# Trunk block on one core: x parts kept in DRAM, retention results transposed on VectorE, squares and last stores regrouped

## The chip, the cores and the metric

The kernel runs on one core of a Trainium2 chip. The metric is the device time of one execution in microseconds (us); lower is better. Engines are named as in the profile: PE (TensorE matmuls), PEld (its weight loads), DVE (VectorE), ACT (ScalarE), POOL (GpSimd), SP (SyncE, which here only issues DMAs).

## What is computed

One layer of a hybrid trunk over 16 meta tokens and 4096 tokens of width 1024, in float32. The reference, cut to what matters:

```python
u = _rmsnorm(h, norm_gain[l])
proj = jnp.einsum('btd,de->bte', u, w_in[l])
lru_x, lru_gate, q, k, v, ret_gate = jnp.split(proj, split_idx, axis=-1)
xc = _causal_conv(lru_x, conv_w[l], conv_b[l])
y_lru = _rg_lru(xc, w_rg[l], b_rg[l], w_ig[l], b_ig[l], lru_lambda[l]) * jax.nn.silu(lru_gate)
...
o = _head_norm(_retention(qh, kh, vh), ret_norm_gain[l])
y_ret = o.reshape(B, T, RET_WIDTH).astype(x.dtype) * jax.nn.silu(ret_gate)
y = jnp.concatenate([y_lru, y_ret], axis=-1)
h = h + jnp.einsum('bte,ed->btd', y, w_out[l])
return _rmsnorm(h, final_norm_gain)[:, N_META:]
```

`_retention` works on chunks of 128 tokens with a state that is handed from chunk to chunk; there are 8 heads of 64 (q, k) and 128 (v) columns.

## The kernel before, in words

Every float32 operand of a large product is held as two parts, `hi` (the value rounded to the matmul's format) and `lo` (the rest), and every product is three matmuls (`mm3`: hi·hi, hi·lo, lo·hi, lines L114 to L116). `split` makes the parts, on ACT (hi, L105) and DVE (lo, L106).

The program has three stages. `ph` is 0 or 1, one half of the channels or heads.

1. **LRU stage**, ph 0 (to about 430 us) and ph 1 (to about 862 us). Tokens go in nine tiles of 272, 256 and seven times 512 columns. `load_x` brings a tile's x in four pairs (`xraw`, 512 KB each, L445) and splits them; the parts of a tile are eight buffers of the pool `big` (28 buffers, 24 of which hold weights and x in use). For each of four blocks `b` of 128 channels PE makes `px` and `pg` (24 matmuls each) and the gate products `pgt`. `block_front` and `block_back` run on ACT and DVE, and `tail` stores the results `sg` to `ydram` (L522).
2. **Retention**, ph 0 (862 to about 1490 us) and ph 1 (to about 2130 us), 32 chunks each. `ret_x` brings the chunk's x once more, from a copy in another order (`xraw` from `xt`, 512 KB), and splits it on ACT (L179) and POOL (L180). A chunk is a pipeline: `front_qk`, `front_v`, `front_g` project it (`ps`), `back_s` makes the scores `pS`, `back_o` the output `po` and the state's update `pkv`, then DVE and POOL take the head norm's statistics, ACT writes `on` (L791), `back_g` multiplies it by the gate (`on` by `gs`, DVE L797), and `back_y` transposes `on` with four PE matmuls against the identity (`py`, L804), copies `py` out on ACT (`yt`, L805) and stores it to `ydram` (256 KB). `back_g` and `back_y` are those of the chunk before the last.
3. **Output sweep** (2130 us to the end): y times w_out, with Strassen-like sums, seven products `i` for each pair of row tiles (a `Unit`). Half h = 0 (LRU channels) adds its rows into `hdram` by an accumulating DMA on POOL's queue; half h = 1 (retention channels, from about 2440 us) adds `hdram` to its rows (`h<-hdram`, L346), then takes their squares (ACT, L348), the root (POOL, L349 and L351), the scaling (DVE, L357) and stores them.

A scheduler that models the engines sets the order of the instructions on each engine; `tc.issue_after` ties some to another. All SP DMAs share one queue in issue order and eight semaphore lanes, so that each waits for the one eight before it.

Of the kernel before, what the change touches and what calls it, by code (L numbers as in the profile page):

```python
# [10 lines left out]
F32 = mybir.dt.float32  # L11
# [22 lines left out]
def hybrid_kernel(ctx: ExitStack, tc: tile.TileContext, xa, xt, x, meta, w_in, w_out,  # L34
# [12 lines left out]
    ydram = [dpool.tile([P, 16, P], F32, name=f"ydram{n}") for n in range(NT)]  # L47
# [97 lines left out]
    rws, rxs = {}, {}  # L145

# [18 lines left out]
    def ret_x(ph, n):  # L165
        if (ph, n) not in rxs:
# [75 lines left out]
    class Unit:  # L242
        def __init__(self, h, n0, n1):
            self.h, self.n, self.y, self.raw = h, (n0, n1), {}, None

        def load(self):
            self.raw = []
            for n in self.n:
                t = raws.tile([P, 2, 4, P], F32, tag="raw", name="yraw")
                load(t, ydram[n][:, 8 * self.h:8 * self.h + 8, :].rearrange("p (g k) t -> p g k t", g=2))  # L250
                self.raw.append(t)

        def operand(self, i):
# [16 lines left out]
            return split(src, t[:, 0], t[:, 1])  # L270
# [29 lines left out]
    def combine(u, i):  # L300
# [13 lines left out]
        if late_unit(u):  # L314
            r0, r1 = u.r
            if i == 2:
# [3 lines left out]
                return add(x0[:, :512], r0[:, :512], g[0])  # L320
# [19 lines left out]
    def finished(u, j, sq):  # L340
# [621 lines left out]
```

## Time and profile before

| what | value |
|---|---|
| median of 3 runs (lowest, highest) | 2776.18 us (2774.13, 2776.66) |
| the profiled execution's own time | 2772.7 us |
| its span (first to last instruction) | 2770.9 us |
| busy: PE | 2716.7 us, 98% of the span |
| busy: DVE, ACT, POOL | 2130.1, 1374.0, 544.9 us (77%, 50%, 20%) |
| moved by DMA | 290.10 MB, mean 105 GB/s |

Busy time of PE is the time in which some matmul is under way. The share of an engine over the whole span hides which stage it belongs to, and a row of the timeline tells when an instruction began, how long it took and, in brackets, how long its engine had stood idle ahead of it and who released it.

### The profile page before, as it was taken

What the parts mean: (1) busy time and instruction counts of PE and PEld (TensorE: products, weight loads), DVE (VectorE), ACT (ScalarE), POOL (GpSimd) and SP (SyncE); (2) the same over time, 40 slices, a digit from 0 to 9 for tenths busy, and PEclk for the clock granted to TensorE, in tenths of its full rate; (3) what the DMA queues carried; (4) which work ended last, traced back from release to release, by engine and by line L of the source; (5) the groups of instructions that cost most, each with busy time, mean ns of one, the idle gap of its engine ahead of it and who ended that gap; (6) DMA issues with size and microseconds to landing.
All of it is one profiled execution on the core that took longest, in us unless ns stands there. A gap on an engine that the chain in (4) does not pass through costs nothing.

```text
span 2770.9 us, 37027 instructions
## 1 busy us (share of the span) xinstructions
PE 2716.7 (98%) x13178; PEld 2288.6 (83%) x13178; DVE 2130.1 (77%) x4502; ACT 1374.0 (50%) x2451; POOL 544.9 (20%) x702
## 2 busy tenths in 40 slices
PE   7999999999999999999999999999999999999998
PEld 7788888888888888888888888888887888877886
DVE  7777889878789877777779888888778755566664
ACT  5766666655565444444446544454445422244342
POOL 3101021000003322222222222222221000012222
PEclk9999999999999999999999999999999999999999
DMA  6434334212224222222214222223112745475654
GB/s 197 120 106 121 118 97 122 84 57 67 75 85 145 72 69 72 69 72 69 70 57 164 79 80 83 101 109 114 47 48 77 191 112 111 108 206 162 178 158 116
DMA packets 164411, 290.10 MB, mean 105 GB/s; under 512 B 21201, under 2 KB 89330, under 8 KB 163714
## 3 DMA queue, kind: packets, MB, share of 16 engines
q1 hardware_dynamic: 150690, 238.45, 26.8%
q0 software_dynamic: 13536, 49.29, 8.2%
q8 instruction: 103, 1.69, 0.3%
q14 instruction: 82, 0.67, 0.1%
HBM read 205.87 MB, written 98.58 MB: 110 GB/s over the span
## 4 chain that ended last, share of the span: by engine, by line
PE 80%; DVE 9%; DMA 4%; issue 3%; ACT 2%; POOL 1%; SPq 0%; DVEq 0%; POOLq 0%; ACTq 0%
PE ps L114 12%; PE ps L116 12%; PE ps L115 12%; PE pg L114 3%; PE pg L116 3%; PE pg L115 3%; PE px L116 3%; PE px L114 3%; PE px L115 3%; PE po L764 2%; PE oc L295 2%; PE oc L297 2%; PE od L297 2%; PE oc L296 2%; PE od L296 2%
## 5 line engine op out<-in xcount | busy, mean ns | idle before, releaser
L114 PE MATMUL ps<-cwh,xhi 128*128 128x512 f32 x1536 | 605.7, 394 | 0.6 <-DVE mr L671 0.6
L116 PE MATMUL ps<-cwh,xlo 128*128 128x512 f32 x1536 | 600.4, 391 | 0.7 <-POOL xlo L180 0.7
L115 PE MATMUL ps<-cwl,xhi 128*128 128x512 f32 x1536 | 600.3, 391 | 0.0
L116 PEld LDWEIGHTS ps<-cwh,xlo 128*128 128x128 f32 x1536 | 288.9, 188 | 62.4 <-POOL xlo L180 1.1
L114 PEld LDWEIGHTS ps<-cwh,xhi 128*128 128x128 f32 x1536 | 289.2, 188 | 57.4 <-DVE mr L671 1.0
L115 PEld LDWEIGHTS ps<-cwl,xhi 128*128 128x128 f32 x1536 | 289.2, 188 | 55.8 <-issue 0.2
L634 DVE STREAM_TRANSPOSE pT<-rd 32x128 f32<-32x128 f32 x1024 | 310.0, 303 | 16.4
L180 POOL TENSOR_TENSOR xlo<-xraw,xhi 128x1024 fp32r<-128x1024 f32 x64 | 163.8, 2559 | 529.6 <-ACT xhi L179 523.6
L105 ACT ACTIVATE yop<-yraw 128x512 fp32r<-128x512 f32 x192 | 116.9, 628 | 217.6 <-DVE yraw L264 71.5
L114 PE MATMUL px<-xhi,lwh 128*128 128x512 f32 (+2 forms) x576 | 215.3, 375 | 8.3 <-ACT lwh L108 6.5
L114 PE MATMUL pg<-xhi,lwh 128*128 128x512 f32 (+2 forms) x576 | 212.8, 370 | 3.6 <-DVE sg L492 3.2
L116 PE MATMUL px<-xhi,lwl 128*128 128x512 f32 (+2 forms) x576 | 214.3, 372 | 1.0 <-DVE lwl L106 1.0
L116 PE MATMUL pg<-xhi,lwl 128*128 128x512 f32 (+2 forms) x576 | 212.4, 369 | 2.8 <-DVE lwl L109 1.7
L115 PE MATMUL px<-xlo,lwh 128*128 128x512 f32 (+2 forms) x576 | 213.9, 371 | 1.0 <-DVE xlo L106 0.9
L115 PE MATMUL pg<-xlo,lwh 128*128 128x512 f32 (+2 forms) x576 | 212.2, 368 | 0.0
L475 DVE SCALAR_TENSOR_TENSOR xc<-xlb,vec,xc 128x512 f32<-128x512 f32 (+2 forms) x216 | 155.4, 720 | 30.2 <-ACT xc L472 26.5
L106 DVE TENSOR_TENSOR yop<-yraw,yop 128x512 fp32r<-128x512 f32 x192 | 130.0, 689 | 52.6 <-ACT yop L105 50.7
L791 ACT ACTIVATE on<-po,nb,rs 128x128 f32<-128x128 f32 x256 | 96.3, 457 | 129.7 <-POOL nb L788 129.7
L782 DVE BATCH_NORM_STATS2 bs<-po 128x6 f32<-128x128 f32 x256 | 57.0, 285 | 108.0 <-PE po L764 107.9
L114 PEld LDWEIGHTS px<-xhi,lwh 128*128 128x128 f32 x576 | 110.5, 192 | 26.8 <-ACT lwh L108 6.5
L114 PEld LDWEIGHTS pg<-xhi,lwh 128*128 128x128 f32 x576 | 109.5, 190 | 22.3 <-DVE sg L492 4.3
L115 PEld LDWEIGHTS px<-xlo,lwh 128*128 128x128 f32 x576 | 110.6, 192 | 20.1 <-DVE xlo L106 1.9
(216 smaller groups left out, 6179.8 us busy)
## 6 DMA issues: line engine op xcount, KB each, us to landing
xraw<-in_xt_dram SPq DMA_DIRECT2D x64, 512.0 KB, 4.6
yraw<-ydram SPq DMA_DIRECT2D x64, 512.0 KB, 3.8
xraw<-in_xa_dram SPq DMA_DIRECT2D x56, 512.0 KB, 4.0
hdram<-in_x_dram SPq DMA_DIRECT2D x32, 512.0 KB, 3.9
xn<-in_x_dram SPq DMA_DIRECT2D x32, 512.0 KB, 5.3
ydram<-sg SPq DMA_DIRECT2D x256, 64.0 KB, 1.7
ydram<-yt SPq DMA_DIRECT2D x64, 256.0 KB, 2.4
hdram<-h POOLq DMA_DIRECT2D x32, 512.0 KB, 5.2
```

Of the source, the lines that this page charges most:

```text
L105: nc.scalar.activation(hi, src, AF.Identity)
L106: return nc.vector.tensor_tensor(lo, src, hi.bitcast(F32), op=ALU.subtract)
L114: nc.tensor.matmul(ps, ah, bh, start=start, stop=False)
L115: nc.tensor.matmul(ps, ah, bl, start=False, stop=False)
L116: nc.tensor.matmul(ps, al, bh, start=False, stop=stop)
L180: nc.gpsimd.tensor_tensor(lo, raw, hi.bitcast(F32), op=ALU.subtract)
L296: nc.tensor.matmul(ps, ah, bl, start=False, stop=False, skip_group_check=more)
L297: mm = nc.tensor.matmul(ps, al, bh, start=False, stop=k == 3, skip_group_check=more)
L475: conv = nc.vector.scalar_tensor_tensor(xc[:, :T], xl[:, j:j + T], vec[:, 6 + j, ch:ch + 1], xc[:, :T], op0=ALU.mult, op1=ALU.add)
L634: ins = nc.vector.transpose(dst[32 * g:32 * g + 32, :, 32 * q:32 * q + 32], sv[32 * q:32 * q + 32, :, g, :])
L782: nc.vector.bn_stats(bs[:, h, :], po[:, h, :])
L791: nc.scalar.activation(on[:, h, :], po[:, h, :], AF.Identity, bias=nb[:, h:h + 1], scale=rs[:, h:h + 1])
```

## The change

Five edits come together.

1. *x parts in DRAM.* The eight parts of each 512-column tile are stored to `xsd` (eight 512 KB DMAs per tile, seven tiles in ph 0; the two small tiles follow in ph 1, `keep_x`). In ph 1 the LRU stage loads the parts of the 512-column tiles from there (two DMAs per pair where there was one, no split), and the retention loads both parts of each chunk (two DMAs of 512 KB in runs of 512 bytes, where there were one DMA, an ACT and a POOL instruction).
2. *Zeros first.* DVE clears a buffer, and PE multiplies it 12 times (128x512) ahead of its first real matmul.
3. *Late squares.* In half h = 1 the squares of a unit are issued after the hi part of the product i = 7 of the next (`added`), the last unit takes half of its squares two products earlier, and the last two row tiles are scaled and stored in two column halves, through SP.
4. *Retention results.* The four PE transposes, the ACT copy and the one 256 KB store give way to one DVE instruction that transposes each 32x32 block of the 128x512 tile, and four stores of 64 KB in runs of 128 bytes that put the blocks in their places in `yret`. The rows of w_out and the head norm's gains are put in the matching order on the host. `back_y` is tied to the same place as `back_g`.
5. *Small loads later.* The loads of `tgm`, `dc`, `msk` and `tg` are tied to the last `xraw` load.

The diff, cut to its core:

```diff
-    ydram = [dpool.tile([P, 16, P], F32, name=f"ydram{n}") for n in range(NT)]
+    ydram = [dpool.tile([P, 8, P], F32, name=f"ydram{n}") for n in range(NT)]
+    yret = [[dpool.tile([P, 4, P], F32, name=f"yret{n}_{ph}") for ph in range(2)] for n in range(NT)]
...
@@ ret_x
-                raw = raws.tile([P, KT, P], F32, tag="raw", name="xraw")
-                nc.sync.dma_start(out=raw, in_=xt[n])
-                hi = big.tile([P, KT, P], F32R, tag="b", name="xhi")
-                lo = big.tile([P, KT, P], F32R, tag="b", name="xlo")
-                nc.scalar.activation(hi, raw, AF.Identity)
-                nc.gpsimd.tensor_tensor(lo, raw, hi.bitcast(F32), op=ALU.subtract)
-                rxs[ph, n] = (hi, lo)
+                i = next(j for j, tt in enumerate(ttiles) if n in tt[2])
+                o = (n - ttiles[i][2][0]) * P + (NM if i == 0 else 0)
+                parts = []
+                for s, nm in enumerate(("xhi", "xlo")):
+                    t = big.tile([P, KT, P], F32R, tag="b", name=nm)
+                    nc.sync.dma_start(out=t.bitcast(F32), in_=xsd[i][s][:, :, o:o + P])
+                    parts.append(t)
+                rxs[ph, n] = tuple(parts)
...
@@ Unit.load
-                load(t, ydram[n][:, 8 * self.h:8 * self.h + 8, :].rearrange("p (g k) t -> p g k t", g=2))
+                if self.h == 0:
+                    load(t, ydram[n].rearrange("p (g k) t -> p g k t", g=2))
+                else:
+                    for ph in range(2):
+                        load(t[:, ph], yret[n][ph])
...
@@ combine, late unit, i == 2
-                return add(x0[:, :512], r0[:, :512], g[0])
+                op = add(x0[:, :512], r0[:, :512], g[0])
+                square(u, 1, 1, g[0])
+                square(u, 0, 0, g[0])
+                return op
...
@@ finished
-        if not late_unit(u):
+        if late_unit(u):
+            square(u, j, 1 - j, sq)
+            root(t, n)
+        else:
             nc.gpsimd.dma_start(out=t, in_=hdram[n], accum_op=ALU.add)
-        for c in range(2):
-            nc.scalar.activation(sq, t[:, 512 * c:512 * c + 512], AF.Square, accum_out=es[:, n, c:c + 1])
+            adding.append((u, j, sq))
...
+    def added(mark, keep=0):
+        while len(adding) > keep:
+            u, j, sq = adding.pop(0)
+            with tc.issue_after(mark.ins):
+                for c in range(2):
+                    square(u, j, c, sq)
+            root(u.x[j], u.n[j])
+
-    def end(keep=0):
-        while len(ending) > keep:
+    def end():
+        while ending:
             t, n = ending.pop(0)
-            nc.vector.scalar_tensor_tensor(t, t, er[:, n:n + 1], gb, op0=ALU.mult, op1=ALU.mult)
-            nc.gpsimd.dma_start(out=out[n * P:(n + 1) * P, :], in_=t)
+            parts = 2 if n >= NT - 2 else 1
+            for c in range(parts):
+                cols = slice(c * D // parts, (c + 1) * D // parts)
+                nc.vector.scalar_tensor_tensor(t[:, cols], t[:, cols], er[:, n:n + 1], gb[:, cols],
+                                               op0=ALU.mult, op1=ALU.mult)
+                (nc.gpsimd if parts == 1 else nc.sync).dma_start(out=out[n * P:(n + 1) * P, cols], in_=t[:, cols])
...
@@ steps of the sweep
-            if i == 5 or (i, u.n[0]) == (6, 4):
+            if i == 7 or (i, u.n[0]) == (1, 4):
+                added(u.hi[i], 2 if i == 1 else 0)
+            if i in ((6, 5) if u.n[0] == 4 else (4,)):
                 with tc.issue_after(op.ins):
-                    end(2 if i == 6 else 0)
+                    end()
...
+    xsd = [[dpool.tile([P, KT, tt[1]], F32, name=f"xs{i}_{s}") for s in range(2)]
+           for i, tt in enumerate(ttiles)]
...
@@ load_x
+            if ph == 1 and i > 1:
+                parts = []
+                for s, nm in enumerate(("xhi", "xlo")):
+                    t = big.tile([P, 2, TB], F32R, tag="b", name=nm)
+                    nc.sync.dma_start(out=t[:, :, :T].bitcast(F32), in_=xsd[i][s][:, kk, :])
+                    parts.append(t)
+                return parts
...
+        def keep_x(i, parts):
+            with tc.issue_after(lloads[-1].ins):
+                for k2, pair in enumerate(parts):
+                    for s, t in enumerate(pair):
+                        store.dma_start(out=xsd[i][s][:, 2 * k2:2 * k2 + 2, :], in_=t[:, :, :ttiles[i][1]].bitcast(F32))
...
@@ LRU stage, first tile and each tile's end
+                    wz = big.tile([P, KT, P], F32R, tag="b", name="wz")
+                    nc.vector.memset(wz[:, 0:4, :].bitcast(F32), 0.0)
+                    pz = psp.tile([P, TB], F32, tag="c", name="pz")
+                    for _ in range(12):
+                        nc.tensor.matmul(pz, wz[:, 0, :], wz[:, 0:4, :], start=True, stop=True)
...
+                if (ph == 0) == (i > 1):
+                    keep_x(i, parts)
...
@@ front_qk
-                with tc.issue_after(nc.sync.dma_start(out=tg, in_=trig[n]).ins):
+                with tc.issue_after(xloads[-1].ins):
+                    tl = nc.sync.dma_start(out=tg, in_=trig[n])
+                with tc.issue_after(tl.ins):
...
@@ back_y
-                yt = mp.tile([P, 4, P], F32, tag="mm", name="yt", bufs=4)
-                py = psp.tile([P, 4, P], F32, tag="c", name="py")
-                for h in range(4):
-                    nc.tensor.transpose(py[:, h, :], on[:, h, :], idf)
-                nc.scalar.copy(out=yt, in_=py)
-                store.dma_start(out=ydram[n][:, 8 + 4 * ph:12 + 4 * ph, :], in_=yt)
+                yt = mp.tile([P, 16, 32], F32, tag="mm", name="yt", bufs=4)
+                nc.vector.transpose(yt.rearrange("p b t -> p (b t)"), on.rearrange("p h d -> p (h d)"))
+                dst = yret[n][ph].rearrange("(e g) k t -> e (g k) t", g=4)
+                for a in range(4):
+                    r = slice(32 * a, 32 * a + 32)
+                    store.dma_start(out=dst[:, :, r], in_=yt[r])
...
@@ host
+    order = np.arange(1024).reshape(2, 4, 4, 32).transpose(0, 2, 3, 1).reshape(-1)
...
+        "w_out": np.concatenate([i["w_out"][0][:LW], i["w_out"][0][LW:][order]]),
```

The order of the instructions, first on PE, in the middle of a retention chunk of ph 0. Before (`pkv` is the last product of `back_o`, `ps0` the first of the next chunk's `front_qk`):

```order
L114 MATMUL pkv_12045<-vh_11773,kn_11734 128x256
L115 MATMUL pkv_12045<-vl_11774,kn_11734 128x256
L116 MATMUL pkv_12045<-vh_11773,kn_11734 128x256
L804 MATMUL py_12083<-idf_259,on_11876 128x128 x4
L114 MATMUL ps0_12099<-cwh_7439,xhi_12092 128x512
L115 MATMUL ps0_12099<-cwl_7440,xhi_12092 128x512
L116 MATMUL ps0_12099<-cwh_7439,xlo_12093 128x512
```

The same place in the changed kernel:

```order
L118 MATMUL pkv_9336<-vh_9068,kn_9029 128x256
L119 MATMUL pkv_9336<-vl_9069,kn_9029 128x256
L120 MATMUL pkv_9336<-vh_9068,kn_9029 128x256
L118 MATMUL ps0_9386<-cwh_7552,xhi_9379 128x512
L119 MATMUL ps0_9386<-cwl_7553,xhi_9379 128x512
L120 MATMUL ps0_9386<-cwh_7552,xlo_9381 128x512
```

The four `py` rows are gone and nothing stands in their place.

On DVE, around `back_g` of a chunk (`pT` transposes q and k, `vl` and `ql` are lo parts, `bs` the statistics of `po`). Before:

```order
L106 TENSOR_TENSOR kn_10934<-rd_10926,kn_10934 128x256
L634 STREAM_TRANSPOSE pT_11009<-rd_10926 32x4x32 x9
L797 TENSOR_TENSOR on_10876<-on_10876,gs_10602 128x512
L106 TENSOR_TENSOR vl_10974<-v_10971,vh_10973 128x512
L106 TENSOR_TENSOR ql_11027<-pT_11009,qh_11026 128x512
L782 BN_STATS bs_11061<-po_11034 128x6 x4
```

In the changed kernel:

```order
L110 TENSOR_TENSOR kn_10597<-rd_10589,kn_10597 128x256
L697 STREAM_TRANSPOSE pT_10672<-rd_10589 32x4x32 x9
L862 TENSOR_TENSOR on_10543<-on_10543,gs_10273 128x512
L110 TENSOR_TENSOR vl_10637<-v_10634,vh_10636 128x512
L867 STREAM_TRANSPOSE yt_10745<-on_10543 128x512
L110 TENSOR_TENSOR ql_10690<-pT_10672,qh_10689 128x512
L797 SCALAR_TENSOR_TENSOR gs_10665<-th_10666,gs_10665 128x512
L847 BN_STATS bs_10724<-po_10697 128x6 x4
```

The `yt` transposition stands ahead of `ql`, and `gs` has moved ahead of the statistics.

On PE, where one 512-column tile of the LRU stage in ph 1 ends and the next begins. Before (`xhi_5707` and `xlo_5708` are the new tile's first pair, `xhi_5713` its second):

```order
L116 MATMUL pgt_5679<-xch_5578,gwl_3999 128x512
L114 MATMUL px_5729<-xhi_5707,lwh_3773 128x512
L115 MATMUL px_5729<-xlo_5708,lwh_3773 128x512
L116 MATMUL px_5729<-xhi_5707,lwl_3774 128x512
L114 MATMUL px_5729<-xhi_5707,lwh_3773 128x512
L115 MATMUL px_5729<-xlo_5708,lwh_3773 128x512
L116 MATMUL px_5729<-xhi_5707,lwl_3774 128x512
L114 MATMUL px_5729<-xhi_5713,lwh_3773 128x512
L114 MATMUL pg_5754<-xhi_5707,lwh_3780 128x512
L115 MATMUL pg_5754<-xlo_5708,lwh_3780 128x512
L116 MATMUL pg_5754<-xhi_5707,lwl_3781 128x512
L115 MATMUL px_5729<-xlo_5714,lwh_3773 128x512
```

In the changed kernel (`xhi_5858` and `xlo_5860` the first pair, `xhi_5862` and `xlo_5864` the second):

```order
L118 MATMUL px_5874<-xhi_5862,lwh_3918 128x512
L118 MATMUL pg_5899<-xhi_5858,lwh_3925 128x512
L119 MATMUL pg_5899<-xlo_5860,lwh_3925 128x512
L120 MATMUL pg_5899<-xhi_5858,lwl_3926 128x512
L118 MATMUL pg_5899<-xhi_5858,lwh_3925 128x512
L119 MATMUL pg_5899<-xlo_5860,lwh_3925 128x512
L120 MATMUL pg_5899<-xhi_5858,lwl_3926 128x512
L119 MATMUL px_5874<-xlo_5864,lwh_3918 128x512
```

Ahead of these rows the changed kernel has the same six `px` matmuls of the first pair behind six `pgt` ones. Three more `pg` matmuls stand ahead of the first use of the second pair's lo part, as for the pairs after it.

## Rows read from the trace of the kernel before

**Rows 1.** Busy time by stretch: us, PE, PEld, DVE, ACT, POOL, granted clock, DMA share, GB/s.

```profile
6.50:21.30 14.80, 12.03 (x48) 11.09 (x49) 14.47 (x42) 11.18 (x25) 8.49 (x8) 1.00 1.07 308
110.00:430.00 320.00, 319.09 (x1398) 262.58 (x1399) 263.52 (x420) 206.85 (x301) 48.56 (x57) 1.00 0.38 110
900.00:1480.00 580.00, 579.79 (x2978) 495.68 (x2978) 455.45 (x1205) 272.81 (x545) 157.08 (x207) 1.00 0.23 73
1509.60:1513.00 3.40, 3.40 (x10) 2.63 (x9) 1.41 (x4) 2.77 (x5) 2.35 (x5) 0.50 0.72 277
2140.50:2144.40 3.90, 3.89 (x9) 3.11 (x10) 1.73 (x3) 3.09 (x8) 0.73 (x1) 0.50 0.02 6
```

**Rows 2.** PE's timeline inside a retention chunk.

```profile
1102.46 0.60 PE L804 MATMUL py<-idf,on 128*128 128x128 f32 x4
1102.82 0.47 PE L114 MATMUL ps<-cwh,xhi 128*128 128x512 f32 x1
1103.14 0.39 PE L115 MATMUL ps<-cwl,xhi 128*128 128x512 f32 x1
1103.37 0.40 PE L116 MATMUL ps<-cwh,xlo 128*128 128x512 f32 x1
```

**Rows 3.** Groups by line: busy us, mean ns of one, idle before.

```profile
L634 DVE STREAM_TRANSPOSE pT<-rd 32x128 f32<-32x128 f32 x1024 | 310.0, 303 | 16.4
...
L180 POOL TENSOR_TENSOR xlo<-xraw,xhi 128x1024 fp32r<-128x1024 f32 x64 | 163.8, 2559 | 529.6 <-ACT xhi L179 523.6 <-PE px L115 6.0
...
L106 DVE TENSOR_TENSOR ql<-pT,qh 128x512 fp32r<-128x512 f32 x64 | 43.8, 685 | 0.0
...
L804 PE MATMUL py<-idf,on 128*128 128x128 f32 x256 | 38.7, 273 | 3.1 <-DVE on L797 1.8 <-ACT qh L105 1.4
```

**Rows 4.** DVE, ACT and PE around the `ql` of one chunk, timelines of the three engines.

```profile
1101.95 0.89 DVE L782 BATCH_NORM_STATS2 bs<-po 128x6 f32<-128x128 f32 x4 [2.44 <-PE po L764]
...
1119.45 0.82 ACT L742 CAST qbl<-ql 64x256 fp32r<-64x256 f32 x2 [0.86 <-DVE ql L106]
...
1128.41 0.28 PE L115 MATMUL pS<-qbl,qh 128*128 128x256 f32 x1
```

**Rows 5.** PE's timeline at the turn from ph 0 to ph 1 of the retention.

```profile
1507.86 0.41 PE L804 MATMUL py<-idf,on 128*128 128x128 f32 x2 [1.38 <-ACT qh L105]
```

**Rows 6.** PE's timeline at the turn from retention to output sweep.

```profile
2135.88 0.63 PE L804 MATMUL py<-idf,on 128*128 128x128 f32 x4 [1.54 <-DVE on L797]
2140.51 0.80 PE L295 MATMUL ob<-owh,yop 128*128 128x512 f32 x1 [4.00 <-ACT yop L105]
```

**Rows 7.** PE's timeline at the start, matmuls of 272 columns.

```profile
20.98 0.43 PE L115 MATMUL pg<-xlo,lwh 128*128 128x272 f32 x1
...
21.54 0.28 PE L115 MATMUL px<-xlo,lwh 128*128 128x272 f32 x1
```

**Rows 8.** PE and SP in ph 1 of the LRU stage: a tile's last `pg`, and the stores before.

```profile
598.89 33.77 SPq L522 DMA_DIRECT2D ydram<-sg  x16
...
634.11 0.39 PE L114 MATMUL pg<-xhi,lwh 128*128 128x512 f32 x1
```

**Rows 9.** DMA issues: count, KB each, median us from issue to landing.

```profile
xraw<-in_xa_dram SPq DMA_DIRECT2D x56, 512.0 KB, 4.0
ydram<-sg SPq DMA_DIRECT2D x256, 64.0 KB, 1.7
mraw<-in_xa_dram SPq DMA_DIRECT2D x2, 64.0 KB, 2.7
rrow<-rstd SPq DMA_DIRECT2D x7, 2.0 KB, 10.2
```

**Rows 10.** PE's timeline in half h = 1 of the sweep.

```profile
2490.26 0.79 PE L295 MATMUL oc<-owh,yop 128*128 128x512 f32 x1 [3.33 <-ACT oc L348]
```

**Rows 11.** ACT and DVE at the end, on the last row tile.

```profile
2759.38 0.60 ACT L348 ACTIVATE od<-h 128x512 f32<-128x512 f32 x1
...
2761.73 1.28 DVE L357 SCALAR_TENSOR_TENSOR h<-h,er,gb 128x1024 f32<-128x1024 f32 x1 [1.94 <-POOL er L351]
```

More of the change, by code (lines that the diff above doesn't have):

```diff
@@ L33, in hybrid_kernel @@
 @with_exitstack
-def hybrid_kernel(ctx: ExitStack, tc: tile.TileContext, xa, xt, x, meta, w_in, w_out,
+def hybrid_kernel(ctx: ExitStack, tc: tile.TileContext, xa, x, meta, w_in, w_out,
                   w_rg, w_ig, vecs, fgain, trig, trigm, mask, dec, ident, out):
@@ L101, in channel_constants @@
         nc.vector.tensor_scalar(cm2, sp, -4.0, None, op0=ALU.mult)
+    hi_op = [None]
     def split(src, hi, lo, scale=None):
         if scale is None:
-            nc.scalar.activation(hi, src, AF.Identity)
+            hi_op[0] = nc.scalar.activation(hi, src, AF.Identity)
             return nc.vector.tensor_tensor(lo, src, hi.bitcast(F32), op=ALU.subtract)
@@ L124, in lru_weight @@
         raw = raws.tile([P, KT, P], F32, tag="raw", name="lraw")
-        nc.sync.dma_start(out=raw, in_=w_lru[:, :, c0:c0 + P])
+        lloads.append(nc.sync.dma_start(out=raw, in_=w_lru[:, :, c0:c0 + P]))
         hi = big.tile([P, KT, P], F32R, tag="b", name="lwh")
@@ L145, in hybrid_kernel @@
     rws, rxs = {}, {}
+    xloads = []
+    lloads = []
     def ret_w(ph, kind, k2):
@@ L243, in __init__ @@
         def __init__(self, h, n0, n1):
-            self.h, self.n, self.y, self.raw = h, (n0, n1), {}, None
+            self.h, self.n, self.y, self.hi, self.raw = h, (n0, n1), {}, {}, None
         def load(self):
@@ L269, in operand @@
             self.y[i] = t
-            return split(src, t[:, 0], t[:, 1])
+            lo = split(src, t[:, 0], t[:, 1])
+            self.hi[i] = hi_op[0]
+            return lo
     def residual(u):
@@ L344, in finished, with square, root @@
             return
-        if not late_unit(u):
+        if late_unit(u):
+            square(u, j, 1 - j, sq)
+            root(t, n)
+        else:
             nc.gpsimd.dma_start(out=t, in_=hdram[n], accum_op=ALU.add)
-        for c in range(2):
-            nc.scalar.activation(sq, t[:, 512 * c:512 * c + 512], AF.Square, accum_out=es[:, n, c:c + 1])
+            adding.append((u, j, sq))
+    adding = []
+    def square(u, j, c, sq):
+        n = u.n[j]
+        nc.scalar.activation(sq, u.x[j][:, 512 * c:512 * c + 512], AF.Square, accum_out=es[:, n, c:c + 1])
+    def root(t, n):
         nc.gpsimd.tensor_scalar(er[:, n:n + 1], es[:, n, 0:1], es[:, n, 1:2], D * EPS,
@@ L440, in load_rb, with load_x @@
             return rb
-        def load_x(i, k2):
+        def load_x(ph, i, k2):
             t0, T, tiles = ttiles[i]
+            kk = slice(2 * k2, 2 * k2 + 2)
+            if ph == 1 and i > 1:
[5 more added lines that the diff above has]
+                return parts
             raw = raws.tile([P, 2, TB], F32, tag="raw", name="xraw")
-            nc.sync.dma_start(out=raw[:, :, :T], in_=xa[:, 2 * k2:2 * k2 + 2, t0:t0 + T])
+            xloads.append(nc.sync.dma_start(out=raw[:, :, :T], in_=xa[:, 2 * k2:2 * k2 + 2, t0:t0 + T]))
             hi = big.tile([P, 2, TB], F32R, tag="b", name="xhi")
             lo = big.tile([P, 2, TB], F32R, tag="b", name="xlo")
-            if i == 0 and k2 >= 2:
+            if ph == 0 and i == 0 and k2 >= 2:
                 nc.scalar.activation(hi[:, :, :T], raw[:, :, :T], AF.Identity)
@@ L532, in get_x @@
             if (ph, i, k2) not in xparts:
-                xparts[ph, i, k2] = load_x(i, k2)
+                xparts[ph, i, k2] = load_x(ph, i, k2)
             return xparts[ph, i, k2]
@@ L812, in hybrid_kernel @@
             xm = ret_x(ph, -1)
-            nc.sync.dma_start(out=tgm[:NM], in_=trigm)
-            nc.sync.dma_start(out=dc, in_=dec[ph])
-            nc.sync.dma_start(out=msk, in_=mask[ph])
+            with tc.issue_after(xloads[-1].ins):
+                nc.sync.dma_start(out=tgm[:NM], in_=trigm)
+                nc.sync.dma_start(out=dc, in_=dec[ph])
+                nc.sync.dma_start(out=msk, in_=mask[ph])
             mk = proj_meta(0, xm, 256)
@@ L877, in hybrid_kernel @@
                     back_g(prev2)
-                with tc.issue_after(mark.ins):
                     back_y(prev2)
@@ L929 @@
     trig, trigm, mask, dec = _tables()
+    order = np.arange(1024).reshape(2, 4, 4, 32).transpose(0, 2, 3, 1).reshape(-1)
     vecs = np.stack([col(i["norm_gain"][0]), col(i["conv_b"][0]), col(i["b_rg"][0]), col(i["b_ig"][0]),
-                     col(i["lru_lambda"][0]), col(i["ret_norm_gain"][0])]
+                     col(i["lru_lambda"][0]), col(i["ret_norm_gain"][0][order])]
                     + [col(i["conv_w"][0, j]) for j in range(4)], axis=1)
@@ L934 @@
         "xa": np.concatenate([i["meta_tokens"], x]).reshape(NM + SEQ, KT, P).transpose(2, 1, 0),
-        "xt": x.reshape(NT, P, KT, P).transpose(0, 3, 2, 1),
         "x": x,
@@ L938 @@
         "w_in": i["w_in"][0],
-        "w_out": i["w_out"][0],
+        "w_out": np.concatenate([i["w_out"][0][:LW], i["w_out"][0][LW:][order]]),
         "w_rg": i["w_rg"][0],
```

## Prediction

> **What bounds the kernel now.** I read the busy time by stretch first. In the LRU stage and in the retention PE is busy 319.09 of 320.00 us and 579.79 of 580.00 us [rows 1], and DVE, the next, 455.45 of 580.00. PE bounds the kernel, nothing else is near, and a gain must be PE time taken out or one of PE's few waits. So I next read PE's timeline inside a retention chunk, for what PE does that is no product of the reference, and then the places where PE stands idle: the start, the turn between the two halves of the retention, the turn to the output sweep, the first squares, and the end. The DMAs come last, since the change adds many of them.
>
> **Transposes off PE (edit 4).** In a chunk the four `py` matmuls begin at 1102.46, the next `ps` at 1102.82, the one after it at 1103.14 and the third at 1103.37 [rows 2]. Matmuls of 512 columns follow each other by 0.23 us (1103.14 to 1103.37), but the first pair is 0.32 apart. So `py` holds PE for 0.36 us and puts off what follows by another 0.09: 0.45 us per chunk, and 64 chunks make **28.8 us**. The bounds are 64 x 0.36 = 23.0 and the group's busy time, 38.7 us [rows 3], which counts overlap with the neighbours. I take 28.8, because starts are what a full PE queue loses. The order shows nothing in the place of `py`.
>
> The transposition now costs DVE one instruction per chunk on 128x512, which the trace does not show. The nearest rows are another 128x512 instruction, 0.69 us (`ql`), and 32x128 transposes of 0.30 us each, four of which have as many columns: 1.21 us [rows 3]. I take 1.2, the row of the same operation. DVE is busy 455.45/580.00 of the time, 15.5 us of a chunk of 19.8 (the 64 chunks lie between 862 and 2130 us), so it fits; it stands ahead of `ql` and the statistics, where DVE had 2.44 us idle waiting for PE [rows 4]. What is queued behind it is `ql`, for which the ACT cast `qbl` waits, and for that `pS`: `qbl` ends at 1119.45 + 0.82 = 1120.27, and `pS` reads it at 1128.41 [rows 4]. That leaves 8 us against 1.2. Cost at the end: nothing; without this cover it would be 64 x 1.2 = 77 us.
>
> The ACT copy goes, and so does the `xlo` of POOL, 2.56 us per chunk [rows 3]; neither was waited for in the middle of a half, so neither is worth anything by itself.
>
> The four stores of 64 KB are 512 runs of 128 bytes each. The nearest rows are 64 KB in long runs, 1.7 us, a load of 64 KB in 1024 runs of 64 bytes, 2.7 us, and 512 writes of 4 bytes, 10.2 us (behind queued 512 KB loads) [rows 9]. I take 2.7: it has more and shorter runs than these. Four in a row are 10.8 us of a 19.4 us chunk. The other transfers of a chunk are three of 512 KB, at 308 GB/s [rows 1] 1.7 us each, 5.1 us. All one after another make 16 us, less than a chunk; nobody on an engine waits for these stores before the sweep. Cost: nothing, with the far end below as a rival. The Trainium skill speaks against this part: "DMA: Bandwidth & Descriptors", Specifications, gives 512 bytes as the least run for line rate, with read-modify-write below it, and its Rules for kernel authors say that a transfer under 64 KB is mostly overhead. By that rule the stores would be slow, but no run here yet shows 128-byte stores, and the row of 64-byte runs, a load, took 2.7 us.
>
> **The two turns.** At the turn from ph 0 to ph 1, PE waited 1.38 us for the buffer of a `py` [rows 5], and then the granted clock was 0.50, the lower level of 1.2 GHz, for 3.40 us [rows 1], where half the time is lost: 1.7. With `py` gone nothing is queued there but `ps`, whose operands lie ready, and ACT, which is late, is next needed for `pS`, about 8 us on. **3.1 us**, from 0 to 3.1. At the turn to the sweep PE waited 1.54 us ahead of `py`, and 4.00 more ahead of `ob` at 2140.51 [rows 6], and ran 3.90 us at a clock of 0.50 [rows 1]. `ob` waits for `yop`, made by DVE and ACT from loaded y; the last `py` and its copy no longer stand between, but the load and the split do. At most 1.54 + 0.63 + 4.00 = 6.2 goes, at least nothing; I take the 1.54 and about a quarter of the rest, **2.5 us**, and the lower clock stays.
>
> **Zeros first (edit 2).** The matmuls at the start take 0.43 us at 20.98 and 0.28 at 21.54 [rows 7], so PE runs at its lower rate for the first 15 us, though the granted clock column reads 1.00 there. If twelve 512-column matmuls end that sooner, the 48 matmuls between 6.5 and 21.3 us take half of their 12.03 us [rows 1], 6.0 us less. But DVE was busy 14.47 of those 14.80 us on the lo parts that PE needs, so most turns into waits. I take **2 us**, from 0 to 6.0. Zeros that ran over the first loads would cost: 12 at the lower rate, 0.43 apart, are 5.2 us, and PE was idle for the 6.5 us before.
>
> **x parts from DRAM (edit 1).** PE's count of matmuls does not change, so in the best case this is worth nothing. Does a load come late? In ph 1 the parts of the next tile go into buffers that the last `pg` of this tile gives back. That `pg` began at 634.11, and SP's stores had been issued by 598.89 + 33.77 = 632.66 [rows 8]: the queue is free. The first buffers are free six matmuls later, at +1.4 us; the first load then takes 4.0 us [rows 9], to +5.4, and the others follow at 1.7 us each: +7.1, 8.8, 10.5, 12.2, 13.9. By the order, 24 `pg`, 6 `pgt` and 6 `px` of the pair already there come ahead of the second pair's hi part: 36 x 0.227 = +8.2; its lo part is wanted at +9.8, and the last two pairs at +11.4, 12.7, 14.3 and 15.9. The slack is 2.0 to 2.8 us everywhere. I take 0. In ph 0 the stores of a tile, 8 x 512 KB in about 50 us, add 85 GB/s to 110 GB/s [rows 1], with a DMA share of 0.38 now: room for them. In the retention two loads of 512 KB per chunk have a whole chunk of 19 us ahead of them.
>
> **Late squares and the end (edits 3, 5).** PE waits 3.33 us ahead of `oc` at 2490.26 for the ACT squares [rows 10], which wait for the accumulating DMA. ACT's and POOL's rows up to these first squares come in the same order before and after, so this wait stays; for smaller ones I take **1 us**, from 0 to 5 (3.33 and the 1.7 of a lower clock). On the last row tile one square of 0.60 with its 0.19 goes from the chain, and the scaling of 1.28 [rows 11] is halved, but the other tile's halves now stand near it on DVE: **1.2 us**, from 0 to 2. Edit 5 takes four DMAs from ahead of the third weight load; it is in the 2 us of the start.
>
> **Sum.** 28.8 + 3.1 + 2.5 + 2 + 1 + 1.2 = 38.6 us from 2772.7, the profiled execution's time (span 2770.9 and 1.8 around it): 2734.1. The median of the runs is 3.5 above the profiled one, so the forecast is 2738.
>
> **Rivals.** *Late loads in ph 1.* If a pair comes some 2 us late in each of the seven tiles, and the clock then falls as at the retention's turn (1.7), it costs 7 x 3.7 = 26 us: 2764. For it: a slack of only 2 us, and 64 KB stores that share the engines. Against it: 308 GB/s were reached, and these loads have no split behind them. *Stores bind the retention* (slower): if four stores take 4t one after another with 5.1 us of other loads, a chunk is longer than the 19.4 that PE needs from t = 3.6 us, and the gain of 38.6, 0.6 per chunk, is gone at t = 3.7. At the far row, t = 10.2, a chunk takes 45.9 us and the time is about 2738 + 64 x 26.5 = 4434; at t = 4.2, a little past that point, 2738 + 64 x 2.5 = 2898. For it: short runs. Against it: 2.7 us for shorter runs, and DMAs that overlap. *The chunk stays as long as it was*: DVE becomes the engine that PE waits for, through the serial path of statistics, state and `ql`, and gives back 0.45 us per chunk, leaving the 9.8 us of the other terms at most: 2766 to 2776. Against it: 4 us of DVE idle time per chunk.
>
> **Numbers.** The forecast 0.73 (by itself 2722 to 2748: gains at their bounds, 51 us, with 3 us for the spread of the runs, and at 28.8 alone), late loads 0.14, binding stores 0.06, an unshortened chunk 0.07. The range 2722 to 2764 leaves out the binding stores and most of the last. A measurement of this kernel tells 0.2%, 5.6 us, from no change. Faster: 0.73, 0.12 of the late loads and 0.03 of the last, 0.88; same 0.05; slower 0.07.
>
> **What would show it.** In the retention a chunk of 19.4 to 19.5 us and no `py`; a DVE transposition of 0.7 to 1.2 us; y stores that land in under 3 us; no PE idle time at `px`, `pg` in ph 1 released by `xhi` or `xlo` DMAs; the wait of 3.3 us ahead of `oc` still there. Wrong would be: PE waits of over 1 us that recur per tile or per chunk.

## The result, and the profile after

The changed kernel takes **2748.44 us** (median of 4 runs, 2744.62 to 2754.78); the kernel before, on the same chip, 2775.15 (2772.87 to 2776.66). The ratio is 0.9909, with a 95% interval of [0.9895, 0.9923]: 25 us less by the ratio (the two medians are 26.7 apart). That is inside the range of 2722 to 2764, 10 us above the forecast of 2738, and at the upper edge of the 2722 to 2748 that the forecast had by itself. The profiled execution took 2744.6 with a span of 2742.8, 28.1 less than before; it is the fastest of the four. Terms below are differences of profiled executions ("by the spans"), and the verdicts on small ones go by the ratios ("by ratio").

Busy time by stretch, columns as in [rows 1]: the start, the LRU stage in ph 0, the retention, and the stretch behind the turn to the sweep, with one more of the start in the last row.

```profile
6.50:21.30 14.80, 8.10 (x40) 7.16 (x41) 14.36 (x42) 11.36 (x27) 8.96 (x11) 0.80 0.85 233
110.00:430.00 320.00, 319.19 (x1399) 261.90 (x1398) 255.23 (x419) 202.35 (x298) 45.50 (x54) 1.00 0.62 185
900.00:1480.00 580.00, 579.07 (x2926) 493.13 (x2925) 454.90 (x1272) 238.02 (x503) 77.63 (x181) 1.00 0.40 102
2118.20:2122.20 4.00, 3.93 (x11) 3.11 (x12) 3.95 (x7) 4.00 (x9) 1.87 (x3) 0.58 0.01 4
15.50:22.30 6.80, 5.27 (x23) 5.28 (x24) 6.66 (x21) 4.84 (x8) 3.83 (x8) 0.50 0.46 152
```

PE is still full in the long stages. POOL's time in the retention has halved (157.08 to 77.63), ACT has lost 35 us, DVE is where it was, with the transposition now in it: `gs` has become shorter (last section). The DMA share in ph 0 went from 0.38 to 0.62 and the traffic from 110 to 185 GB/s, near the 195 of the forecast.

PE's timeline at the end of a retention chunk, to set against [rows 2]:

```profile
1082.44 0.28 PE L120 MATMUL pkv<-vh,kn 128*128 128x256 f32 x1
1082.56 0.40 PE L118 MATMUL ps<-cwh,xhi 128*128 128x512 f32 x1
1082.79 0.39 PE L119 MATMUL ps<-cwl,xhi 128*128 128x512 f32 x1
```

No `py` stands between `pkv` and `ps`, and they follow each other at 0.12 and 0.23 us. The groups of DVE by line: the transposition, and the gate product `gs`.

```profile
L867 DVE STREAM_TRANSPOSE yt<-on 128x512 f32<-128x512 f32 x64 | 45.0, 703 | 0.1
...
L797 DVE SCALAR_TENSOR_TENSOR gs<-th,gs 128x512 f32<-128x512 f32 x64 | 44.2, 690 | 111.4 <-ACT gs L796 111.4
```

The transposition takes 0.70 us, and PE never waits for it. `gs` now waits for ACT, which costs nothing. DMA issues of the whole program, columns as in [rows 9]:

```profile
xhi<-xs SPq DMA_DIRECT2D x92, 512.0 KB, 4.7
xlo<-xs SPq DMA_DIRECT2D x92, 512.0 KB, 5.8
...
yret<-yt SPq DMA_DIRECT2D x256, 64.0 KB, 2.2
```

The stores in runs of 128 bytes land in 2.2 us. PE's waits by what is waited for: total us, times, the longest one.

```profile
PE pg L118 <- DVE sg L548: 7.1, 3, 4.1
PE ob L308 <- ACT yop L109: 7.0, 1, 7.0
PE pgt L118 <- ACT xch L109: 6.9, 5, 4.2
PE pg L120 <- DVE lwl L113: 4.6, 1, 4.6
PE px L118 <- DVE xlb L525: 4.2, 1, 4.2
PE oc L308 <- ACT oc L372: 3.3, 1, 3.3
```

Nearly all of it stands at an edge of a stage: the start, the turn from ph 0 to ph 1, the turn to the sweep, the first squares. None is a load of x parts in ph 1: over the whole program the only wait of PE that a DMA of parts releases is 0.9 us, once, in the retention. The 3.3 us ahead of `oc` are still there, as forecast.

To see where the time went I took the same matmul in two traces, by its name and its order, and subtracted the starts (us, against before; three experiments stand beside it, the last of them from another chip, where before took 2777.03):

| mark (time in before) | changed | edit 4 alone | without edit 1 | without edit 3 |
|---|---|---|---|---|
| `px`, ph 0 (135.48) | +2.67 | -1.49 | -1.03 | +2.94 |
| `px`, past the turn to ph 1 (542.38) | +6.55 | -1.09 | -1.37 | +8.24 |
| first `ps` of the retention (839.97) | +6.47 | -1.09 | -1.37 | +8.16 |
| `ps`, ahead of the retention's turn (1482.41) | -8.89 | -14.54 | -15.97 | -7.20 |
| `ps`, four chunks on (1569.51) | -13.16 | -17.93 | -19.35 | -12.10 |
| `ps`, near the end (2046.71) | -23.48 | -28.25 | -29.67 | -22.42 |
| `oc`, sweep half 0 (2372.53) | -24.13 | -28.25 | -29.71 | -23.02 |
| `oc`, end of half 1 (2725.07) | -25.60 | -20.55 | -32.93 | -17.06 |
| span (2770.9) | -28.1 | -20.5 | -35.4 | -17.0 |

In the steady retention the difference grows by 0.44 us per chunk in ph 0 and 0.43 in ph 1: that is edit 4. The changed kernel enters the retention 6.47 us late, and the column without edit 1 does not: 7.8 us lie between them. Half 1 of the sweep is where the columns part again.

### The profile page after: what moved, and what is told of

Its sections match the earlier page's. It is cut to its first block, busy times and chain, and to the rows that moved or that the text cites. A ratio compares the mean times of both kernels' runs of the same rounds, so it can differ in the third digit from the quotient of the medians.

```text
span 2742.8 us, 36798 instructions
## 1 busy us (share of the span) xinstructions
PE 2687.7 (98%) x12934; PEld 2262.3 (82%) x12934; DVE 2062.1 (75%) x4543; ACT 1251.8 (46%) x2297; POOL 347.8 (13%) x634
## 4 chain that ended last, share of the span: by engine, by line
PE 84%; DVE 6%; DMA 4%; issue 2%; ACT 2%; POOL 1%; SPq 0%; DVEq 0%; POOLq 0%; ACTq 0%
PE ps L119 13%; PE ps L118 13%; PE ps L120 13%; PE pg L118 3%; PE pg L120 3%; PE pg L119 3%; PE px L118 3%; PE px L120 3%; PE px L119 3%; PE po L829 2%; PE oc L308 2%; PE oc L310 2%; PE oc L309 2%; PE od L310 2%; PE od L309 2%
## 5 line engine op out<-in xcount | busy, mean ns | idle before, releaser
L118 PE MATMUL ps<-cwh,xhi 128*128 128x512 f32 x1536 | 599.3, 390 | 0.0
L531 DVE SCALAR_TENSOR_TENSOR xc<-xlb,vec,xc 128x512 f32<-128x512 f32 (+2 forms) x216 | 153.5, 712 | 22.2 <-ACT xc L528 19.0
L120 PEld LDWEIGHTS pg<-xhi,lwl 128*128 128x128 f32 x576 | 109.6, 190 | 22.4 <-DVE lwl L113 4.8
L797 DVE SCALAR_TENSOR_TENSOR gs<-th,gs 128x512 f32<-128x512 f32 x64 | 44.2, 690 | 111.4 <-ACT gs L796 111.4
```

The lines of the kernel that those rows point to most:

```text
L118: nc.tensor.matmul(ps, ah, bh, start=start, stop=False)
L120: nc.tensor.matmul(ps, al, bh, start=False, stop=stop)
L531: conv = nc.vector.scalar_tensor_tensor(xc[:, :T], xl[:, j:j + T], vec[:, 6 + j, ch:ch + 1], xc[:, :T], op0=ALU.mult, op1=ALU.add)
```

## Experiments

All ratios are against the kernel before on the same chip. stores_only, double_tr, early_small and raw_turn ran on a slower chip (before took 2787.31 us there), so only their ratios are set against the others; among themselves their times compare.

**Edit 4 alone (before_tr): the transposition and its stores put into the kernel before.**

```diff
-                py = psp.tile([P, 4, P], F32, tag="c", name="py")
-                for h in range(4):
-                    nc.tensor.transpose(py[:, h, :], on[:, h, :], idf)
-                nc.scalar.copy(out=yt, in_=py)
+                nc.vector.transpose(yt.rearrange("p b t -> p (b t)"), on.rearrange("p h d -> p (h d)"))
```

> The kernel before with edit 4 alone (block transposition on DVE, four small stores, rows of w_out reordered). If the transposition carries the whole gain, as I hold, each retention chunk is shorter by 0.43 to 0.45 us, the wait at the turn between the halves of the retention goes, and the time is 27 to 31 us under the kernel before, so as fast as the changed kernel or 1 to 5 us faster. Rival, that the gain needs the other edits too (POOL's and ACT's splits gone from the retention): under 20 us.

2750.97 us, 0.9913 [0.9898, 0.9927]: 24 us, less than expected. Up to half 0 of the sweep it has gained 28.25, as expected, then half 1 gives 7.7 back. PE's waits by what is waited for:

```profile
PE oc L300 <- DVE h L315: 6.9, 8, 1.7
PE oc L300 <- ACT oc L353: 4.1, 1, 4.1
```

Before, `oc` waited 2.0 us for DVE's `h`; now 6.9, in eight places. The accumulating loads stand in the DMA issues with a landing of 6.7 us, where before they took 6.0:

```profile
h<-hdram POOLq DMA_DIRECT2D x30, 512.0 KB, 6.7
```

**One load of y in place of two (before_tr_1load).** Edit 4 also splits each load of y in half 1 into two of 256 KB. Here both halves lie in one tile, loaded at once.

```diff
-                    for ph in range(2):
-                        load(t[:, ph], yret[n][ph])
+                load(t, (ydram, yret)[self.h][n].rearrange("p (g k) t -> p g k t", g=2))
```

> The kernel before with edit 4 alone, but with both halves of a row tile's retention results in one DRAM tile, so that the sweep loads them by one DMA of 512 KB, not two of 256 KB. If the 7.7 us that the sweep's second half lost with edit 4 come from these doubled loads (the accumulating DMAs landed 0.7 us later), 5 to 8 us faster than with two loads, some 2744 us. If they come from the order of the instructions or from elsewhere, within 2 us of 2751.

2751.13 us, 0.9906 [0.9892, 0.9919], the same as with two loads, and `oc` still waits 5.3 us for `h`, in seven places. So the number of loads is not what half 1 loses its time to.

**Without edit 1 (raw_x): x loaded raw and split on chip everywhere, as before.**

```diff
-                if (ph == 0) == (i > 1):
-                    keep_x(i, parts)
```

> The changed kernel without edit 1: x is loaded raw and split in ph 1 and in the retention as before, no parts are stored to DRAM. If the shortfall comes from the DMA traffic of the parts, 4 to 8 us faster than the changed kernel, with the stalls at 60 to 85 us and at 440 us shorter and runs that differ less. If the shortfall sits in instruction order on DVE (extra lo parts at the turn from ph 0 to ph 1, order at the sweep's turn), within 2 us of it.

2739.92 us, 0.9870 [0.9855, 0.9885]: below the changed kernel's interval, about 11 us faster by ratio (0.0039 x 2775), 7.3 by the spans. Edit 1 costs time here. The same stretch of ph 0 without it, and then the DMA issues in it, of the changed kernel and of this one:

```profile
110.00:430.00 320.00, 320.00 (x1404) 263.23 (x1403) 262.76 (x425) 206.35 (x300) 47.91 (x55) 1.00 0.40 111
```

```profile
xs<-xhi SPq DMA_DIRECT2D x23, 512.0 KB, 3.8
xs<-xlo SPq DMA_DIRECT2D x23, 512.0 KB, 6.8
xraw<-in_xa_dram SPq DMA_DIRECT2D x21, 512.0 KB, 5.7
...
ydram<-sg SPq DMA_DIRECT2D x96, 64.0 KB, 2.9
```

```profile
xraw<-in_xa_dram SPq DMA_DIRECT2D x21, 512.0 KB, 3.9
...
ydram<-sg SPq DMA_DIRECT2D x100, 64.0 KB, 2.1
```

The stores of parts lengthen the loads of x beside them from 3.9 to 5.7 us, and the stores of `sg` from 2.1 to 2.9, at a mean share of only 0.62.

**Stores of parts kept, but never read (stores_only).** Edit 1 with its loads taken back: every later use loads raw x again.

```diff
-            if ph == 1 and i > 1:
-                parts = []
...
-                return parts
```

> The changed kernel with the stores of x parts kept, but with x loaded raw and split in ph 1 and in the retention as before; nothing reads what is stored. If the stores alone make the LRU stage 8 us longer, it is as slow as the changed kernel, some 8 us slower than without edit 1. If the loads of the parts are the cost, it is as fast as without edit 1.

0.9894 [0.9879, 0.9908] (2758.5 against 2787.31): 0.0024 or 6.7 us behind raw_x. The two intervals just overlap, and the chips differ; on the same chip raw_turn below, which has no edit 1 either, took 2748.9, 9.6 us less. So the stores are the larger part of what edit 1 costs.

**The stores on POOL's queue (xs_pool).**

```diff
-                        store.dma_start(out=xsd[i][s][:, 2 * k2:2 * k2 + 2, :], in_=t[:, :, :ttiles[i][1]].bitcast(F32))
+                        nc.gpsimd.dma_start(out=xsd[i][s][:, 2 * k2:2 * k2 + 2, :], in_=t[:, :, :ttiles[i][1]].bitcast(F32))
```

> The changed kernel with the stores of x parts issued by POOL on its own queue, not by SP. Without edit 1 the LRU stage was 7.9 us shorter. If the cost comes from the place of these stores on SP's queue, ahead of weight, x and y transfers, most of it goes: 4 to 8 us faster than the changed kernel. If it comes from their bytes on the shared DMA engines, it stays: within 2 us.

2751.03 us, 0.9904 [0.9891, 0.9918], no change, and `xraw` lands in 6.6 us there. It is not the place of the stores in SP's queue. That the transfers meet behind the queues is what is left, not shown by itself.

**The lo parts of ph 1's first tile back on POOL (pool_lo).**

```diff
-            if ph == 0 and i == 0 and k2 >= 2:
+            if i == 0 and k2 >= 2:
```

> The changed kernel with one condition put back: the lo parts of the third and fourth pair of the first tile of ph 1 on POOL again, not on DVE. If these two instructions (1.11 and 1.82 us) on a full DVE are what made the turn from ph 0 to ph 1 3.8 us longer, the PE wait of 4.2 us at 441 us falls to about 2.4 and the time by 2 to 3 us. If the stores of x parts in that place are the cause, nothing changes.

2748.7 us, 0.9904 [0.9887, 0.9920]. The 3.9 us lost at the turn from ph 0 to ph 1 stayed (3.8), so the two lo parts do not make them (the changed kernel also moved these to DVE, which the list of its edits does not name).

**No zeros (no_zeros): edit 2 left out.**

```diff
-                    for _ in range(12):
-                        nc.tensor.matmul(pz, wz[:, 0, :], wz[:, 0:4, :], start=True, stop=True)
```

> The changed kernel without the twelve matmuls with zeros. The changed kernel reached the second block of the first tile 1.6 us earlier than before, and lost that again by 75 us, where PE waits for the row of norms (rb). If the zeros save time only ahead of that wait, the time is the same within 1 us. If they are worth what I forecast, 2 us slower; if the early matmuls push DVE and DMA work out of step (stalls of 4.6 us at 12 and 4.2 us at 60), 2 to 3 us faster.

2748.08 us, 0.9905 [0.9890, 0.9920]: the zeros are worth nothing that can be measured.

**Without edit 3 (plain_squares): squares in their old places.**

```diff
-                square(u, 1, 1, g[0])
-                square(u, 0, 0, g[0])
...
-            if i == 7 or (i, u.n[0]) == (1, 4):
-                added(u.hi[i], 2 if i == 1 else 0)
+            if i == 5 or (i, u.n[0]) == (6, 4):
```

> The changed kernel without edit 3 (squares, scaling and last stores as before). With the transposition alone the sweep's second half became 7.7 us longer and its end was not shorter; in the changed kernel that half was 1.5 us shorter and the end 2.5. If edit 3 is what makes the difference, this kernel is 9 to 12 us slower than the changed one. If edit 3 is worth what I forecast (1 and 1.2 us), about 2 us slower.

2760.38 us, 0.9933 [0.9920, 0.9946]: 6.7 us slower by ratio, 11 by the spans (the intervals just overlap; xs_pool, on the same chip, took 2751.03). Half 1 loses 6.0 us instead of gaining 1.5 and the end gains nothing. The wait is that of edit 4 alone:

```profile
PE oc L308 <- DVE h L323: 7.2, 9, 1.7
```

**One store of 256 KB per chunk (one_store).** Runs of 512 bytes; the blocks are not put in their places, so the sweep works on y in another order.

```diff
-                for a in range(4):
-                    r = slice(32 * a, 32 * a + 32)
-                    store.dma_start(out=dst[:, :, r], in_=yt[r])
+                store.dma_start(out=yret[n][ph], in_=yt.rearrange("p (k a) t -> p k (a t)", k=4))
```

> The changed kernel with one 256 KB store of the transposed blocks in runs of 512 bytes, where there were four of 64 KB in runs of 128 bytes; the blocks are not put in their places, so this leaves that rearrangement out. I hold that the short runs cost nothing: within 1.5 us of the changed kernel, the chunk unchanged. If the short runs press on the DMA engines, 3 us or more faster.

2746.18 us, 0.9887 [0.9872, 0.9902]; the chunk is 19.45 us with either, and the span (2745.0) is no shorter. The intervals overlap: undecided. What does show is the DMA share in the retention, at equal traffic:

```profile
900.00:1480.00 580.00, 580.00 (x2931) 494.26 (x2931) 454.95 (x1275) 236.37 (x500) 77.82 (x181) 1.00 0.35 102
```

0.35 against 0.40 in the changed kernel. The four stores in short runs take 5% more of the DMA engines' time in this stage than the one, and the chunk is no longer for it.

**The transposition twice (double_tr).**

```diff
+                nc.vector.transpose(yt.rearrange("p b t -> p (b t)"), on.rearrange("p h d -> p (h d)"))
```

> The changed kernel with each DVE block transposition done twice (the same result). The transposition took 0.71 us. If DVE hides it in the retention, as the forecast says, a chunk stays at 19.4 us and the time within 1.5 us of the changed kernel. If DVE is close to being waited for, up to 64 x 0.7 = 45 us more.

0.9911 [0.9896, 0.9926] (2764.13 against 2787.31), and the chunk stays at 19.45 us. DVE, with 45 us more, costs nothing: it does not bound the retention. This trace shows a late load of x as well, in ph 0. PE's timeline, and the window around it:

```profile
296.31 0.79 PE L118 MATMUL px<-xhi,lwh 128*128 128x512 f32 x1 [2.68 <-ACT xhi L109]
296.90 0.63 PE L118 MATMUL pg<-xhi,lwh 128*128 128x512 f32 x1
297.33 0.63 PE L119 MATMUL pg<-xlo,lwh 128*128 128x512 f32 x1
```

```profile
290.00:340.00 50.00, 47.32 (x195) 38.13 (x194) 38.88 (x64) 31.40 (x46) 5.76 (x8) 0.93 0.63 194
```

At the start of a tile PE waits 2.68 us for the split of a raw load, and its matmuls then follow each other at 0.43 us, not 0.23 (the granted clock of the 50 us is 0.93). It happens three times (5.9 us of waiting between 200 and 460); in the changed kernel's own trace it does not. Between 130 and 420 us six traces with edit 1 have such a wait for the split of x, of 0.7 us or more (plain_squares, xs_pool, one_store, stores_only, double_tr, early_small); those of the changed kernel, pool_lo and no_zeros have none, nor has any trace without edit 1.

**Without edit 5 (early_small): the retention's small loads free to go ahead of x.**

```diff
-                with tc.issue_after(xloads[-1].ins):
-                    tl = nc.sync.dma_start(out=tg, in_=trig[n])
+                tl = nc.sync.dma_start(out=tg, in_=trig[n])
```

> The changed kernel without edit 5: the small loads are not tied to the last raw load and may be issued at the start again. I forecast nothing by itself for this edit: within 2 us. If the loads at the start delay the third weight load as in the kernel before, 2 to 4 us slower in the first 60 us.

0.9852 [0.9837, 0.9867] (2747.97): faster than the changed kernel, against what I expected. Its trace has one missed load of x (1.7 us) where double_tr has three. On the same chip it is 16 us faster than double_tr, which has the changed kernel's instructions in the same order up to 900 us, and as fast as raw_turn, which has no edit 1. At the first `ps` of the retention it is 15.0 us ahead of double_tr and 1.1 behind raw_turn. So on this chip the cost of edit 1 comes of edits 1 and 5 together; on the others early_small was not run. Why, stays open: between 160 and 438 us every engine has the same instructions in the same order with edit 5 and without, and yet double_tr loses 8.8 us more there. The loads that edit 5 moves, with one 512 KB store behind them, come by 11 us or at 447 to 453.

**Without edit 1, and the gate products and transpositions of the last two chunks behind the sweep's first operands (raw_turn).**

```diff
+                elif n == NT:
+                    held = prev2
...
+                    back_g(held)
+                    back_y(held)
+                with tc.issue_after(mark.ins):
                     back_g(prev2)
                     back_y(prev2)
```

> The changed kernel without edit 1, and with the last two chunks' gate products and transpositions tied behind the sweep's first operands on DVE. At the turn PE waited 7.0 us for the operand yop, since DVE took these instructions first, one of them 2.3 us idle. If that order is the cause, the wait shrinks to 2 to 4 us, with some 2 us lost ahead of the last state product, and the time is 2 to 4 us under the kernel without edit 1. If the loads of y or ACT end the wait, nothing changes.

0.9862 [0.9845, 0.9879] (2748.9): not told apart from raw_x. The 7.0 us ahead of `ob` are gone, but `po` now waits 1.7 us for ACT's `sbh`, 2.0 for DVE's `sbl` and 0.9 for `sm`, and `od` 1.8 for its weights. By the marks 0.5 us is gained.

## Why the prediction was right, and where it was not

**Transposes off PE: right.** Forecast 28.8; measured 32 x 0.443 + 32 x 0.43 = 27.9. The transposition was priced at 1.2 us and took 0.70, as the other 128x512 row; hidden either way, which double_tr shows. The binding stores are refuted: 2.2 us each, where 3.7 would have eaten the gain. The Trainium skill, "DMA: Bandwidth & Descriptors", Specifications, puts the least run for line rate at 512 bytes. The trace agrees in the engines' share (0.40 with four stores in runs of 128 bytes, 0.35 with one in runs of 512) and not in the landing: the four stores of 64 KB land in 2.2 us each, the one of 256 KB in 2.1. The rule of the Trainium skill that the prediction sets beside it, in Rules for kernel authors of the same page, is for transfers under 64 KB, and these are not under it.

**The turn in the retention: right.** Over the four chunks across it the difference grows by 4.27 us (8.89 to 13.16), of which the chunks are 1.72: 2.5, forecast 3.1.

**"Room for them": the step that failed.** The sum gave edit 1 no cost, because a share of 0.38 leaves room on the mean for 85 GB/s more. The traffic came as forecast. What I left out is that the transfers beside these stores land later, and that the start and the turn between the phases have no slack for that. The start was to gain 2 and lost 2.7 (without edit 1 it gains 1.0), and the turn to ph 1 lost 3.9 (without edit 1 it gains 0.3). DVE's timeline ahead of that turn, and then PE's in it:

```profile
403.03 0.69 DVE L548 TENSOR_TENSOR sg<-pg,rb 128x512 f32<-128x512 f32 x1 [2.04 <-PE px L119]
...
418.66 0.69 DVE L548 TENSOR_TENSOR sg<-pg,rb 128x512 f32<-128x512 f32 x1 [1.60 <-DMA ydram<-sg]
```

```profile
420.71 0.40 PE L118 MATMUL pgt<-xch,gwh 128*128 128x512 f32 x1
421.64 0.51 PE L119 MATMUL pgt<-xcl,gwh 128*128 128x512 f32 x1 [0.53 <-DVE xcl L110]
...
445.63 1.22 PE L118 MATMUL pgt<-xch,gwh 128*128 128x512 f32 x2 [4.16 <-ACT xch L109]
```

`sg` needs a buffer that an earlier store of `sg` gives back, and waits for it at 418.66. At 403.03 the row names PE, but it is the same wait: the last `pg` matmul that this `sg` reads began at 395.84 and took 0.39, and the four stores of the `sg` five before it (there are five buffers), issued at 396.85 to 398.21 behind the stores of parts, landed at 402.10 to 402.81. Without edit 1 the same `sg` starts at 393.88 without a wait. The landing of these four stores, in the changed kernel and then without edit 1:

```profile
DMA to landing us min/median/max: 4.6/5.0/5.2
```

```profile
DMA to landing us min/median/max: 1.6/1.7/1.7
```

So DVE's second `sg` starts 2.05 us ahead of the `pgt` at 420.71; without edit 1 it is 5.79 (410.63 to 416.42). From there DVE works without a gap, and PE reaches the turn first.

SP's queue isn't the cause (xs_pool); that the bytes meet on the shared DMA engines is argued from the landing times. Nor is it edit 1 by itself: edit 5, which the sum had in the 2 us of the start, has a part in it, since early_small, with edit 1 and without edit 5, shows no such cost. The rival of late loads named ph 1, where nothing came late; its mechanism showed up in ph 0, at the tile starts of double_tr.

**The turn to the sweep: sign wrong.** Forecast -2.5, measured +1.1 (four chunks should have gained 1.72 between the last two marks of the retention and half 0, and 0.65 came). The wait ahead of `ob` grew from 4.00 to 6.96 us, because PE reaches it sooner and the operands do not (with the 1.54 that PE had waited ahead of `py`, it was 5.54). DVE's timeline ahead of it:

```profile
2112.09 0.69 DVE L862 TENSOR_TENSOR on<-on,gs 128x512 f32<-128x512 f32 x1 [2.34 <-ACT on L856]
2112.81 0.71 DVE L867 STREAM_TRANSPOSE yt<-on 128x512 f32<-128x512 f32 x1
2113.45 1.25 DVE L273 TENSOR_TENSOR s<-yraw 128x512 f32<-128x512 f32 x2
2114.62 0.88 DVE L847 BATCH_NORM_STATS2 bs<-po 128x6 f32<-128x128 f32 x4
2115.42 1.27 DVE L274 TENSOR_TENSOR yraw<-yraw 128x512 f32<-128x512 f32 x2
```

I had taken the last `py` and its ACT copy for what stood between. It is DVE: its queue still holds the last normalization (2.34 us idle for ACT), the transposition and the statistics ahead of the additions that make `yop`. raw_turn moved this work, and the wait went to other operands.

**Zeros: 2 us forecast, none measured.** The matmuls did run faster sooner: those of 272 columns follow each other at 0.12 to 0.13 us by 7.3 us, where before they needed 0.23 up to 21.2. But PE then waits 4.6 us for the weights' lo part (`lwl` in the list of waits), and the granted clock is 0.50, the lower level of 1.2 GHz, from 15.5 to 22.3 us (last row of the first block above), so that they need 0.23 again up to 22.2. What is left is lost at 64 us: DVE waits for a load, `rb`, till 64.11 (64.75 before), and PE for DVE 4.2 us, where it was 2.0 and 0.9.

**Late squares: undersized.** 1 us in half 1 forecast; they are worth 7.4 there by the spans (+6.0 without, -1.5 with) and 2.5 more at the end (1.2 forecast). By ratio edit 3 is worth 6.7 in all. They do not shorten the kernel before by that much: they repair what edit 4 does to half 1. Edit 4's accumulating loads land 0.7 us later, and `oc` waits for the sums behind them. Why they land later I could not find: it isn't the number of loads of y, and the engines' order in half 1 is the same. Open.

Sum of the profiled times: lost 6.5 up to ph 1, gained 27.9, 2.5 at the turn and 1.2 in the other chunks of the retention, lost 1.1, gained 1.5 and 2.5: 28.0 of the 28.1. The forecast for that execution was 38.6. That the time fell inside the range is in part luck: the loss that edit 4 brings to half 1 was not foreseen, nor that edit 3 would make up for nearly all of it, and the range reached past 2748 only for late loads in ph 1 and an unshortened chunk, which did not come.

**The best versions** are the changed kernel without edit 5 (0.9852) and without edit 1 (0.9870, or 0.9862 in raw_turn), 36 to 41 us less than before. Their intervals overlap, and leaving out both was not tried.

## What to carry to other kernels

Price an added transfer by what it does to the landing of the loads beside it, at the points where those have no slack (the start, turns, tile starts), and not by mean bandwidth. An engine that is full gives back what is taken from it, instruction by instruction; look then for the chain that was just in time before, because PE will reach it sooner. Try the parts of a change apart: here a sum that was still a gain hid two parts, and leaving out either one gained another 11 to 16 us by ratio.

## What the runs showed of the hardware

DVE's `gs` took 1627 ns in the median before and 693 in the changed kernel, with the same shape. These are the instructions of that line: duration min/median/max in ns, first and last start; before, then without edit 1, then changed.

```profile
L732 DVE SCALAR_TENSOR_TENSOR gs<-th,gs x64: 651/1627/2027, 883.8 to 2128.8; 128x512 f32<-128x512 f32 x64
```

```profile
L785 DVE SCALAR_TENSOR_TENSOR gs<-th,gs x64: 650/1842/2855, 881.0 to 2101.3; 128x512 f32<-128x512 f32 x64
```

```profile
L797 DVE SCALAR_TENSOR_TENSOR gs<-th,gs x64: 657/693/694, 885.9 to 2107.4; 128x512 f32<-128x512 f32 x64
```

The slow two have POOL's 2.56 us subtraction `xlo` in each chunk; the quick one has not. In the kernel before, the 50 of the 64 `gs` that overlap an `xlo` took 1612 to 2027 ns, and the 14 that overlap none 651 to 693. The Trainium skill, "SBUF — State Buffer", Who interferes with whom, says that a DVE instruction with two SBUF inputs contends with a GpSimd instruction that reads SBUF; the trace agrees. It was worth nothing here, since DVE does not bound the retention.
